# Six raw weight buffers, group results in two wide tiles, and gate operands parked by chunk in a decoder trunk on one core

## The chip, the core and the metric

The kernel runs on one core of one Trainium2 chip. The metric is the device time of one execution in microseconds (us). A core has a matrix engine (TensorE, PE in the profile; its weight loads are PEld), a vector engine (VectorE, DVE), a scalar engine (ScalarE, ACT), GpSimd (POOL) and a queue engine (SyncE, SP). Each runs its own instructions in order and waits for the others by semaphores. Here SP issues nearly all loads, POOL the copies of intermediate results to and from DRAM.

## What is computed

Two layers, each with one input projection that feeds three causal token mixers, and a merge; then a final norm. `D_MODEL` is 2048, the sequence 256 tokens. Cut to what matters:

```python
h = rms_norm(x, norm_w)
proj = h @ w_in                      # 2048 x 18064, float32
(qa, ka, va, za, qi, ki, wi, ub, zb, qc, kc, vc, zc, gates) = split(proj)
y_a = (dsa_attention(rope(qa), rope(ka), va, rope(qi), rope(ki), wi, top_k) * silu(za)) @ w_a_out
y_b = (silu(layer_norm(conv31(glu(ub)))) * silu(zb)) @ w_b_out
y_c = (stick_breaking_attention(qc, kc, vc) * silu(zc)) @ w_c_out
g = sigmoid(gates).reshape(b, s, 3, D_MODEL)
merged = g[:, :, 0] * y_a + g[:, :, 1] * y_b + g[:, :, 2] * y_c
x = x + merged @ w_out
```

## The kernel before

**Weights.** Weights stream from DRAM in units of 512 KB: `load_unit` (L179) takes a raw tile (tag `raw`, four buffers), `high` (L202) rounds it to `wh` on ACT, `low` (L206) forms the rest `wl` on DVE. The operands have three buffers each. A product then takes three passes over PE: high by high, high by low, low by high. A unit of eight or twelve matmuls of 512 columns belongs to `chunk_T` (L221), `chunk_first` (L253) or `chunk_steps` (L280).

**Slots.** Activations live in slots (tag `s8`, 128 x 2048 float32, 13 buffers; L92), smaller ones in `t4` tiles (128 x 1024, six buffers; L123). A slot is as large as two raw tiles.

**Background work.** The attention parts are generators. `background` (L142) steps at most one of the first two after each weight unit; the number that a generator yields is how many units must be loaded before its next step. `finish` runs out what is left. The taps of the depthwise convolution (L358: four products on ACT, one add on DVE) stand in a list `waiting`, from which `drain` takes one entry after each `low`; empty entries (L611) space them out.

**Stages of a layer.** Conv input and taps; stick-breaking queries, keys, values; then `stick` (L633) beside the sparse attention's projections; `index` (L708) and `attend` (L749) beside four gate chunks of branch 1 (`early`); `conv_norm` (L796) beside the gated operands. `gate` (L349) builds the gated operand of a branch in two slots, high and low parts side by side. Those of branches 2 and 0 are parked in DRAM (`park`, L790), to free their slots, and read back by `unpark` (L853).

**Merge stage.** `combine` (L859) runs over the branches in the order 1, 2, 0. Chunks of 512 gate columns are computed plainly, or read back from DRAM if they are done. The gates of branch 0 are computed by `strassen` (L935): seven products for eight, on sums of two weight blocks that `summands` (L923, the DVE add at L926) forms from raw tiles. The loop at L995 alternates: after each step of `combine` it lets the groups run on by two units of their yields. A group's four results stand in one slot, `res` (L959), and go to DRAM at L988. `turn` and the output projection follow; the rows of x that it adds are loaded on SP (L1020, L1022).

A scheduler orders each engine's instructions by the program's order, by raised priorities, and by its own estimate of when a tile is free. So the number of buffers changes the order too.

Of the kernel before, what the change touches and what calls it, by code (L numbers as in the profile page):

```python
# [8 lines left out]
F32 = mybir.dt.float32  # L9
F32R = mybir.dt.float32r  # L10
AF = mybir.ActivationFunctionType
ALU = mybir.AluOpType
# [37 lines left out]
def trunk(ctx: ExitStack, tc: tile.TileContext, x, xt, w_in, w_a, w_b, w_c, w_out,  # L50
# [37 lines left out]
    def nm(s):  # L88
        uid[0] += 1
        return f"{s}_{uid[0]}"  # L90

    def slot(dt=F32):  # L92
        return sp.tile([P, KC, S], dt, tag="s8", bufs=13, name=nm("s8"))

# [19 lines left out]
    def split_at(b, k, n, src, ts=slice(0, S)):  # L114
        split(hi(b, k, n, ts), lo(b, k, n, ts), src)
# [63 lines left out]
    def load_unit(w, k0, kn, segs, dst=None):  # L179
        n = sum(c for _, c in segs)  # L180
        raw = wp.tile([P, kn, n], F32, tag="raw", bufs=4, name=nm("raw"))
        if dst is None:
# [165 lines left out]

    def gate(c0, o, b, w, hx):  # L349
        for k in range(0, KC, 2):  # L350
            a, a3 = summed(chunk_T(w, c0 + k * P, 256, hx, KD))
            sg = sigmoid_of(a)
            with tc.high_priority():
                nc.vector.tensor_mul(a3, a3, sg)
                nc.vector.tensor_mul(a3, a3, o[:, k:k + 2, :])
                split_at(b, k, 2, a3)

    def taps(yT, cv, pr, c0, q):  # L358
# [42 lines left out]
    x1 = dp.tile([NT, P, D], F32, name="x1")  # L401
    parked = [[dp.tile([P, 4, 2, S], F32R, name=f"parked{b}{i}") for i in range(2)] for b in range(3)]
    gates = [dp.tile([NT, P, D], F32, name=f"gates{b}") for b in range(3)]
# [14 lines left out]
    for layer in range(DEPTH):  # L418
# [177 lines left out]
        for j in range(2):  # L596
# [11 lines left out]
            for q in reversed(range(TAPS)):  # L608
                waiting.append([4, [partial(taps, yT, cv, pr, j * 4, q)]])
                if q % 2:  # L610
                    waiting.append([4, []])  # L611
# [21 lines left out]
        def stick(h0, qcT=qcT, kcT=kcT, vcr=vcr, diag=diag):  # L633
# [20 lines left out]
            split(*pr_, nk[:, :768])  # L654
            yield 8
            pc = mm_tile()
# [92 lines left out]
        def attend(t, c, qaT=qaT, kaT=kaT, va=va, bias=bias):  # L749
# [24 lines left out]
            split(ph[:, :4 * n], pl[:, :4 * n], pst[:, :4 * n])  # L774
            yield 2
            po = mm_tile()
# [11 lines left out]
        for j in range(2, 4):  # L788
            early(1, j)
        def park(b, g):  # L790
            for i, v in enumerate(g):
                nc.gpsimd.dma_start(parked[b][i], v)

        finish()
        flush()
        def conv_norm(cv=cv, pr=pr):  # L796
            work = t4()
            red = [work[:, i * S:(i + 1) * S] for i in range(4)]
            sums = red[2:]
            for i in range(2):  # L800
                nc.vector.tensor_reduce(red[i], cv[:, i * 4:i * 4 + 4, :].rearrange("p c t -> p t c"), op=ALU.add, axis=AX.X)  # L801
            nc.vector.tensor_add(red[0], red[0], red[1])
            yield 3
            ps = mm_tile()
            nc.tensor.matmul(ps[:, :S], mean_w, red[0], start=True, stop=True)
            for i in range(2):
                cs = cv[:, i * 4:i * 4 + 4, :]
                nc.vector.tensor_sub(cs, cs, heads(ps[:, :S], 4))
                sq = t4()
                nc.scalar.activation(sq.rearrange("p (c t) -> p c t", c=4), cs, AF.Square)  # L810
                nc.vector.tensor_reduce(sums[i], sq.rearrange("p (c t) -> p t c", c=4), op=ALU.add, axis=AX.X)
            nc.vector.tensor_add(sums[0], sums[0], sums[1])
            yield 6
            vs = mm_tile()
            nc.tensor.matmul(vs[:, :S], mean_w, sums[0], start=True, stop=True)
            r = rsqrt_mean(vs[:, :S], 1, t4())
# [11 lines left out]
        gc = parts(KC)  # L828
        gate(O_ZC, qcT, gc, w, hx)
        park(2, gc)  # L830
        ga = parts(KC)
        gate(O_ZA, qaT, ga, w, hx)
        park(0, ga)
        finish()
# [16 lines left out]
        mx = [None] * 4  # L851

        def unpark(b):  # L853
            g = parts(KC)
            for i, v in enumerate(g):
                nc.gpsimd.dma_start(v, parked[b][i])
            return g
# [77 lines left out]
        def strassen(b, jj):  # L935
# [4 lines left out]
            for u in range(4):  # L940
# [17 lines left out]
                yield 2  # L958
            res = slot().rearrange("p a b -> p (a b)").rearrange("p (q t d) -> p q t d", q=2, t=NT)  # L959
            c11, c21, c12, c22 = res[:, 0, 0], res[:, 0, 1], res[:, 1, 0], res[:, 1, 1]  # L960
            with tc.high_priority():
# [18 lines left out]
            with tc.high_priority():  # L980
                nc.vector.tensor_add(c11, o2, c11)
                nc.vector.tensor_add(c21, o4, c21)
                nc.vector.tensor_add(c12, o3, c12)
                nc.scalar.activation(res[:, 0], res[:, 0], AF.Sigmoid)
                nc.scalar.activation(c12, c12, AF.Sigmoid)
            for q in range(2):
                j = jj * 2 + q
                nc.gpsimd.dma_start(gates[b][:, :, j * 512:(j + 1) * 512].rearrange("t p d -> p t d"), res[:, q])  # L988
            yield 3
# [5 lines left out]
        for _ in plainly:  # L995
            owed += RATE
            while owed >= 0 and fast_:
                try:
                    owed -= next(fast_[0])
                except StopIteration:  # L1000
                    fast_.pop(0)
# [126 lines left out]
```

## Time and profile before

| | us |
|---|---|
| median of three runs | 2088.27 |
| lowest, highest | 2085.84, 2090.1 |
| profiled execution, whole | 2091.38 |
| its span | 2089.6 |
| mean granted TensorE clock | 0.996 of full |

The span runs from the first to the last instruction of the program; the whole time has some 2 us more around it. A row of a list of groups gives source line, engine, operation, output and input tiles by the program's names, shape, count, then busy time and mean duration (ns), then the idle time of that engine just before and what ended it. A row of waits reads "who waited <- for whom: total us, times, longest us". L-numbers are lines of the kernel before.

### The profile page before, as it was taken

To read this page: it belongs to the slowest core of one execution; us is meant where nothing else is said; L and a number is where in the kernel's file an instruction comes from. 1 tells how busy PE (TensorE), PEld (TensorE's weight loads), DVE (VectorE), ACT (ScalarE), POOL (GpSimd) and SP (SyncE) were. 2 spreads that over 40 slices of the span, in tenths; PEclk is the share of its full clock that TensorE was granted. 3 is DMA by queue.
4 is the path that set the end of the run, shared out by engine and by line. 5 is a ranking of instruction groups with operands and counts; after the bars stand their busy time and mean duration, and the time that the engine had idled before them with its cause. 6 is when DMAs were issued, how large, how long until landed. Compare 5 with 4: busy or idle time off the path is not lost.

```text
span 2089.6 us, 29031 instructions
## 1 busy us (share of the span) xinstructions
PE 2052.1 (98%) x10942; PEld 1778.3 (85%) x10942; DVE 1595.5 (76%) x1828; ACT 1301.4 (62%) x1845; POOL 34.7 (2%) x56
## 2 busy tenths in 40 slices
PE   9999999999999999899999999999999999999998
PEld 9888889988888777788898888899888887787887
DVE  8877677798977878666577777778989678887655
ACT  6887565688655555444459875666876555555444
POOL 0000000000000000000000000000000000000000
PEclk9999999999999999999999999999999999999999
DMA  6666556655776767686666665565557766686864
GB/s 242 204 190 191 167 164 206 202 185 169 242 233 218 238 215 244 227 283 202 204 192 190 185 191 173 162 212 192 187 166 252 231 223 233 225 279 201 275 213 145
DMA packets 302044, 436.24 MB, mean 209 GB/s; under 512 B 17744, under 2 KB 182096, under 8 KB 299728
## 3 DMA queue, kind: packets, MB, share of 16 engines
q1 hardware_dynamic: 293472, 398.20, 60.0%
q0 software_dynamic: 6912, 33.56, 4.5%
q10 hardware_dynamic: 1520, 2.64, 0.4%
q8 instruction: 85, 1.39, 0.3%
q14 instruction: 55, 0.45, 0.1%
HBM read 413.37 MB, written 20.97 MB: 208 GB/s over the span
## 4 chain that ended last, share of the span: by engine, by line
PE 87%; DMA 5%; DVE 5%; issue 2%; ACT 1%; ACTq 0%; SPq 0%; DVEq 0%
PE acc L218 79%; DMA raw<-in_w_in_dram 5%; PE mm L218 4%; DVE wl L208 3%; PE mm L717 1%; ACT wh L204 1%; DVE t L926 1%; PE mm L754 1%; DVE t L801 0%; PE mm L845 0%; PE mm L672 0%; PE mm L636 0%; PE mm L779 0%; PE mm L386 0%; PE mm L658 0%
## 5 line engine op out<-in xcount | busy, mean ns | idle before, releaser
L204 ACT CAST wh<-raw 128x1024 fp32r<-128x1024 f32 (+2 forms) x712 | 740.2, 1040 | 604.7 <-PE acc L218 384.0
L208 DVE TENSOR_TENSOR wl<-raw,wh 128x1024 fp32r<-128x1024 f32 (+2 forms) x713 | 857.8, 1209 | 333.3 <-ACT wh L204 315.6
L218 PE MATMUL acc<-wh,s 128*128 128x512 f32 (+2 forms) x2688 | 652.9, 385 | 0.0
L218 PE MATMUL acc<-s,wh 128*128 128x512 f32 (+2 forms) x2912 | 645.0, 365 | 2.3 <-ACT s L503 1.7
L218 PEld LDWEIGHTS acc<-wh,s 128*128 128x128 f32 x2688 | 492.9, 189 | 96.7 <-ACT wh L204 0.5
L218 PEld LDWEIGHTS acc<-s,wh 128*128 128x128 f32 x2912 | 491.3, 190 | 63.9 <-ACT s L503 2.0
L218 PEld LDWEIGHTS acc<-s,wl 128*128 128x128 f32 x2656 | 357.5, 191 | 19.4 <-DVE wl L208 0.9
L218 PE MATMUL acc<-s,wl 128*128 128x256 f32 (+1 forms) x2656 | 366.1, 281 | 0.5 <-DVE wl L208 0.4
L218 PE MATMUL acc<-wl,s 128*128 128x512 f32 (+2 forms) x1344 | 351.9, 384 | 13.2 <-DVE wl L208 13.1
L218 PEld LDWEIGHTS acc<-wl,s 128*128 128x128 f32 x1344 | 247.2, 188 | 66.5 <-DVE wl L208 18.5
L369 ACT ACTIVATE t<-s,cst 128x255 f32<-128x255 f32 (+14 forms) x480 | 201.5, 489 | 0.2
L372 DVE TENSOR_TENSOR s<-s,t 128x1020 f32<-128x1020 f32 (+14 forms) x120 | 138.3, 1153 | 1.0 <-ACT t L369 0.5
L218 PE MATMUL mm<-wh,s 128*128 128x512 f32 x448 | 119.9, 389 | 0.0
L218 PEld LDWEIGHTS mm<-wh,s 128*128 128x128 f32 x448 | 84.0, 188 | 18.0 <-issue 0.4
L218 PE MATMUL mm<-wl,s 128*128 128x512 f32 x224 | 70.2, 394 | 7.3 <-DVE wl L208 7.3
L204 ACT CAST wh<-s 128x1024 fp32r<-128x1024 f32 x32 | 33.6, 1050 | 47.7 <-DVE s L926 28.4
L218 PEld LDWEIGHTS mm<-wl,s 128*128 128x128 f32 x224 | 41.2, 188 | 19.1 <-DVE wl L208 11.2
L926 DVE TENSOR_TENSOR s<-s,raw 128x1024 f32<-128x1024 f32 x16 | 19.6, 1226 | 46.5 <-DMA raw<-in_w_in_dram 46.5
L926 DVE TENSOR_TENSOR t<-raw,raw 128x1024 f32<-128x1024 f32 x32 | 39.1, 1222 | 16.7 <-DMA raw<-in_w_in_dram 16.7
L204 ACT CAST wh<-t 128x1024 fp32r<-128x1024 f32 x32 | 33.5, 1048 | 19.0 <-DVE t L926 10.5
L208 DVE TENSOR_TENSOR wl<-t,wh 128x1024 fp32r<-128x1024 f32 x32 | 39.0, 1219 | 1.1 <-ACT wh L204 0.7
L208 DVE TENSOR_TENSOR wl<-s,wh 128x1024 fp32r<-128x1024 f32 x32 | 38.9, 1217 | 0.0
(203 smaller groups left out, 1167.5 us busy)
## 6 DMA issues: line engine op xcount, KB each, us to landing
raw<-in_w_in_dram SPq DMA_DIRECT2D x571, 512.0 KB, 3.6
raw<-in_w_out_dram SPq DMA_DIRECT2D x64, 512.0 KB, 3.8
raw<-in_w_b_dram SPq DMA_DIRECT2D x32, 512.0 KB, 3.6
raw<-in_w_c_dram SPq DMA_DIRECT2D x32, 512.0 KB, 5.3
raw<-in_w_a_dram SPq DMA_DIRECT2D x32, 512.0 KB, 5.7
parked<-s POOLq DMA_DIRECT2D x8, 1024.0 KB, 5.5
t<-gates POOLq DMA_DIRECT2D x16, 512.0 KB, 6.4
s<-parked POOLq DMA_DIRECT2D x8, 1024.0 KB, 8.4
```

Source lines behind the costliest of these rows:

```text
L204: nc.scalar.copy(u[1], u[0])
L208: sub = nc.vector.tensor_sub(u[2], u[0], u[1].bitcast(F32))
L218: newest[0] = nc.tensor.matmul(o, lhsT, rhs, start=start, stop=stop, skip_group_check=True)
L369: nc.scalar.activation(o[:, i, :S - d], yT[:, c, :S - d], AF.Copy, scale=wq)
L372: nc.vector.tensor_add(to, to, o[:, :, :S - d])
L717: nc.tensor.matmul(ps[:, q * n:(q + 1) * n], at(qiT, hd)[:, t * P:(t + 1) * P], kiT[:, 0, :n], start=True, stop=True)
L754: nc.tensor.matmul(ps[:, q * n:(q + 1) * n], qaT[:, c * 4 + q, ts_], kaT[:, c, :n], start=True, stop=True)
L926: nc.vector.tensor_tensor(o, a_, b_, op=op)
```

## The change

Raw tiles get six buffers, slots twelve. A group's results go to two `t4` tiles. `gate` parks each pair of chunks as soon as it is formed, into one DRAM tile per branch that is laid out by chunk; `unpark` puts eight small reads on a list, of which the loop of the merge stage issues one per step. The strided reductions of `conv_norm` become adds of halves. `stick` waits 10 units, not 8, before its second step, `attend` 3, not 2, before its third. The empty entries among the taps stand after every fourth tap, not after every second.

```diff
-        return sp.tile([P, KC, S], dt, tag="s8", bufs=13, name=nm("s8"))
+        return sp.tile([P, KC, S], dt, tag="s8", bufs=12, name=nm("s8"))
...
-        raw = wp.tile([P, kn, n], F32, tag="raw", bufs=4, name=nm("raw"))
+        raw = wp.tile([P, kn, n], F32, tag="raw", bufs=6, name=nm("raw"))
...
-    def gate(c0, o, b, w, hx):
+    def gate(c0, o, b, w, hx, park=None):
         for k in range(0, KC, 2):
...
                 split_at(b, k, 2, a3)
+            if park is not None:
+                nc.gpsimd.dma_start(park[:, k:k + 2], part(b, slice(0, 2), k, 2))
...
-    parked = [[dp.tile([P, 4, 2, S], F32R, name=f"parked{b}{i}") for i in range(2)] for b in range(3)]
+    parked = [dp.tile([P, KC, 2, S], F32R, name=f"parked{b}") for b in range(3)]
...
-                if q % 2:
+                if q % 4 == 0:
                     waiting.append([4, []])
...
-            yield 8
+            yield 10
             pc = mm_tile()
...
-            yield 2
+            yield 3
             po = mm_tile()
...
-            for i in range(2):
-                nc.vector.tensor_reduce(red[i], cv[:, i * 4:i * 4 + 4, :].rearrange("p c t -> p t c"), op=ALU.add, axis=AX.X)
-            nc.vector.tensor_add(red[0], red[0], red[1])
+
+            def fold(w_, first, second):
+                w4 = w_.rearrange("p (c t) -> p c t", c=4)
+                nc.vector.tensor_add(w4, first, second)
+                nc.vector.tensor_add(w_[:, :512], w_[:, :512], w_[:, 512:])
+                nc.vector.tensor_add(w_[:, :S], w_[:, :S], w_[:, S:2 * S])
+                return w_[:, :S]
+
+            s1 = fold(work, cv[:, :4, :], cv[:, 4:, :])
             yield 3
...
-        gate(O_ZC, qcT, gc, w, hx)
-        park(2, gc)
+        gate(O_ZC, qcT, gc, w, hx, parked[2])
         ga = parts(KC)
-        gate(O_ZA, qaT, ga, w, hx)
-        park(0, ga)
+        gate(O_ZA, qaT, ga, w, hx, parked[0])
...
+        back = []
+
         def unpark(b):
             g = parts(KC)
-            for i, v in enumerate(g):
-                nc.gpsimd.dma_start(v, parked[b][i])
+            back.extend(partial(nc.gpsimd.dma_start, g[k // 4][:, k % 4], parked[b][:, k]) for k in range(KC))
             return g
...
-            res = slot().rearrange("p a b -> p (a b)").rearrange("p (q t d) -> p q t d", q=2, t=NT)
-            c11, c21, c12, c22 = res[:, 0, 0], res[:, 0, 1], res[:, 1, 0], res[:, 1, 1]
+            res = [t4().rearrange("p (t d) -> p t d", t=NT) for _ in range(2)]
+            c11, c21, c12, c22 = (r[:, t, :] for r in res for t in range(NT))
...
         for _ in plainly:
             owed += RATE
+            if back:
+                back.pop(0)()
```

The squares in `conv_norm` are summed by `fold` in the same way.

**The readbacks, on POOL, in the merge stage of layer 0.** `s` are slots, `parked` and `gates` the tiles in DRAM, `t` the t4 tiles. Before:

```order
L856 DMA s_1081_6695<-parked_87 128x2048
L856 DMA s_1082_6696<-parked_88 128x2048
L988 DMA gates_89<-s_1136_6948 128x2x512 x2
L871 DMA t_1401_8233<-gates_89 128x2x512
L871 DMA t_1415_8312<-gates_89 128x2x512
L856 DMA s_1335_7891<-parked_83 128x2048
L856 DMA s_1336_7892<-parked_84 128x2048
L988 DMA gates_89<-s_1315_7789 128x2x512 x2
```
Now (line numbers of the changed kernel):

```order
L998 DMA s_1081_6696<-parked_85 128x512 x4
L998 DMA s_1082_6697<-parked_85 128x512 x4
L988 DMA gates_86<-t_1136_6955 128x2x512
L988 DMA gates_86<-t_1137_6956 128x2x512
L998 DMA s_1337_7900<-parked_83 128x512 x4
L998 DMA s_1338_7901<-parked_83 128x512 x4
L871 DMA t_1403_8248<-gates_86 128x2x512
L871 DMA t_1417_8327<-gates_86 128x2x512
```
Each readback of a slot is now four transfers that stand side by side; those of branch 0 (`parked_83`) moved ahead of the two reads of finished gates.

**The end of the attention stage in layer 0, on DVE.** `cv` is slot 76; `pl` is the low half of the transposed attention weights, for the last two of four `attend`. Before:

```order
L326 TENSOR_TENSOR pl_4947<-mm_4937,ph_4946 128x1024
L372 TENSOR_TENSOR s_76_720<-s_76_720,t_780_4956 128x4x226
L208 TENSOR_TENSOR wl_5060<-raw_5058,wh_5059 128x1024
L801 TENSOR_REDUCE t_793_5032<-s_76_720 128x256 x2
L326 TENSOR_TENSOR pl_4984<-mm_4974,ph_4983 128x1024
L802 TENSOR_TENSOR t_793_5032<-t_793_5032 128x256
```
Now:

```order
L799 TENSOR_TENSOR t_793_5029<-s_76_717 128x1024
L208 TENSOR_TENSOR wl_5057<-raw_5055,wh_5056 128x1024
L800 TENSOR_TENSOR t_793_5029<-t_793_5029 128x512
L801 TENSOR_TENSOR t_793_5029<-t_793_5029 128x256
L326 TENSOR_TENSOR pl_4968<-mm_4958,ph_4967 128x1024
L208 TENSOR_TENSOR wl_5079<-raw_5077,wh_5078 128x1024
L326 TENSOR_TENSOR pl_4993<-mm_4983,ph_4992 128x1024
```
The reductions and a tap stood between the two `pl`; the adds now stand ahead of the first, and only one low half of a weight unit is left between them.

**The loads on SP before the output projection of layer 0.** Before:

```order
L193 DMA raw_8236<-in_w_a_dram 128x2x512
L193 DMA raw_8254<-in_w_a_dram 128x2x512
L1020 DMA t_1471_8594<-in_x_dram 128x2x512
L193 DMA raw_8272<-in_w_a_dram 128x2x512
L1020 DMA t_1501_8771<-in_x_dram 128x2x512
```
Now:

```order
L193 DMA raw_8251<-in_w_a_dram 128x2x512
L193 DMA raw_8269<-in_w_a_dram 128x2x512
L193 DMA raw_8287<-in_w_a_dram 128x2x512
L193 DMA raw_8305<-in_w_a_dram 128x2x512
L1022 DMA t_1473_8609<-in_x_dram 128x2x512
L193 DMA raw_8330<-in_w_a_dram 128x2x512
L1022 DMA t_1503_8786<-in_x_dram 128x2x512
```
Two more raw loads stand ahead of the first x load. The t4 tiles that the x loads fill are now those of the last group's results, so each waits until its store to `gates` has landed.

More of the change, by code (lines that the diff above doesn't have):

```diff
@@ L789, in trunk @@
             early(1, j)
-        def park(b, g):
-            for i, v in enumerate(g):
-                nc.gpsimd.dma_start(parked[b][i], v)
         finish()
@@ L797, in conv_norm @@
             work = t4()
-            red = [work[:, i * S:(i + 1) * S] for i in range(4)]
-            sums = red[2:]
-            for i in range(2):
-                nc.vector.tensor_reduce(red[i], cv[:, i * 4:i * 4 + 4, :].rearrange("p c t -> p t c"), op=ALU.add, axis=AX.X)
-            nc.vector.tensor_add(red[0], red[0], red[1])
+            def fold(w_, first, second):
[5 more added lines that the diff above has]
+            s1 = fold(work, cv[:, :4, :], cv[:, 4:, :])
             yield 3
             ps = mm_tile()
-            nc.tensor.matmul(ps[:, :S], mean_w, red[0], start=True, stop=True)
+            nc.tensor.matmul(ps[:, :S], mean_w, s1, start=True, stop=True)
+            sq = [t4().rearrange("p (c t) -> p c t", c=4) for _ in range(2)]
             for i in range(2):
@@ L808, in conv_norm @@
                 nc.vector.tensor_sub(cs, cs, heads(ps[:, :S], 4))
[L809 to L812, printed above, removed]
+                nc.scalar.activation(sq[i], cs, AF.Square)
+            s2 = fold(work, *sq)
             yield 6
             vs = mm_tile()
-            nc.tensor.matmul(vs[:, :S], mean_w, sums[0], start=True, stop=True)
+            nc.tensor.matmul(vs[:, :S], mean_w, s2, start=True, stop=True)
             r = rsqrt_mean(vs[:, :S], 1, t4())
@@ L851, in trunk @@
         mx = [None] * 4
+        back = []
         def unpark(b):
             g = parts(KC)
-            for i, v in enumerate(g):
-                nc.gpsimd.dma_start(v, parked[b][i])
+            back.extend(partial(nc.gpsimd.dma_start, g[k // 4][:, k % 4], parked[b][:, k]) for k in range(KC))
             return g
@@ L983, in strassen @@
                 nc.vector.tensor_add(c12, o3, c12)
-                nc.scalar.activation(res[:, 0], res[:, 0], AF.Sigmoid)
+                nc.scalar.activation(res[0], res[0], AF.Sigmoid)
                 nc.scalar.activation(c12, c12, AF.Sigmoid)
@@ L987, in strassen @@
                 j = jj * 2 + q
-                nc.gpsimd.dma_start(gates[b][:, :, j * 512:(j + 1) * 512].rearrange("t p d -> p t d"), res[:, q])
+                nc.gpsimd.dma_start(gates[b][:, :, j * 512:(j + 1) * 512].rearrange("t p d -> p t d"), res[q])
             yield 3
```

## The prediction

> **What bounds the kernel now.** I read the page first, for the engine that is never idle, then the waits of that engine, then the stretches in which those waits lie, then the instructions of one such stretch.
>
> ```profile
> span 2089.6 us, 29031 instructions
> PE 2052.1 (98%) x10942; PEld 1778.3 (85%) x10942; DVE 1595.5 (76%) x1828; ACT 1301.4 (62%) x1845; POOL 34.7 (2%) x56
> PE 87%; DMA 5%; DVE 5%; issue 2%; ACT 1%; ACTq 0%; SPq 0%; DVEq 0%
> ```
> TensorE (PE) is busy 98% of the span, and the chain that ended last runs over it for 87%. The change adds and removes no matmul, so all that it can win is PE's idle time, 37.5 us, and what that idle time costs beside it. The profiled execution took 2091.4 us, 1.8 us more than its span, and lies 3.1 us above the median of the three runs, 2088.3; I make the sum against 2091.4 and take the 3.1 us off at the end.
>
> The list of waits over the whole span says for what PE stood still:
>
> ```profile
> PE acc L218 <- DVE wl L208: 13.5, 10, 4.1
> PE mm L218 <- DVE wl L208: 7.3, 7, 1.6
> DVE s L926 <- DMA raw<-in_w_in_dram: 55.6, 25, 8.3
> SPq L193 <- DVE wl L208: 1487.3, 657, 10.2
> ```
> Columns are total, times and longest. PE waited 17 times, 20.8 us in all, for the low half of a weight unit (`wl`). Behind it VectorE (DVE) stood 55.6 us at the sums of two weight blocks (L926) because a raw block had not landed. And the queue that issues the raw loads (SP) spent 1487 us waiting for DVE to be done with an older raw tile: loads go out late because no raw buffer is free, not because the transfers are slow.
>
> Where those waits lie, by stretches (length, then busy time and instructions of PE, PEld, DVE, ACT, POOL, then granted clock, DMA share and GB/s):
>
> ```profile
> 240.00:330.00 90.00, 88.70 (x550) 80.24 (x549) 68.61 (x89) 61.41 (x81) 0.00 (x0) 1.00 0.55 167
> 430.00:540.00 110.00, 108.85 (x540) 91.75 (x539) 98.69 (x139) 88.33 (x163) 3.47 (x5) 1.00 0.58 182
> 675.00:895.00 220.00, 208.47 (x898) 168.40 (x897) 173.85 (x165) 114.53 (x117) 5.30 (x8) 0.99 0.70 232
> 1280.00:1370.00 90.00, 89.14 (x554) 81.02 (x553) 69.41 (x90) 60.62 (x80) 0.00 (x0) 1.00 0.57 173
> 1470.00:1575.00 105.00, 103.85 (x516) 87.47 (x514) 94.51 (x129) 84.04 (x157) 2.92 (x4) 1.00 0.58 181
> 1710.00:1930.00 220.00, 210.96 (x911) 170.88 (x911) 175.61 (x166) 115.69 (x118) 5.20 (x8) 0.99 0.70 232
> ```
> The merge stage, where the plain chunks and the seven-product groups alternate, holds 11.5 us of idle PE in the first layer and 9.0 in the second: all of the 20.8 us. The stick-breaking and sparse-attention stages hold 1.3 + 1.15 + 0.9 + 1.15 = 4.5 us. The other 12 us of the 37.5 lie outside these stretches, most at the start and behind the last matmul, and I leave them as they are.
>
> The longest wait, in order of time (start, length, engine, operation, in brackets the idle time before it):
>
> ```profile
> 834.93 0.57 POOL L856 DMA_DIRECT2D s<-parked  x1 [25.34 <-PE mm L218]
> 837.83 0.37 SPq L193 DMA_DIRECT2D raw<-in_w_in_dram  x1
> 839.01 0.55 POOL L856 DMA_DIRECT2D s<-parked  x1 [3.51 <-PE mm L218]
> 840.77 0.37 SPq L193 DMA_DIRECT2D raw<-in_w_c_dram  x1
> ...
> 849.03 1.23 DVE L926 TENSOR_TENSOR s<-s,raw 128x1024 f32<-128x1024 f32 x1 [8.29 <-DMA raw<-in_w_in_dram]
> 851.44 2.04 PE L218 MATMUL acc<-wl,s 128*128 128x512 f32 x4 [4.12 <-DVE wl L208]
> ...
> 1885.39 1.78 PE L218 MATMUL acc<-wl,s 128*128 128x512 f32 x4 [3.15 <-DVE wl L208]
> ```
> Two parked tiles of 1 MB each are read back just when three raw loads are under way; the block issued at 837.83 is what L926 waits for until 849.03, and PE loses 4.12 us. The second layer has the like, 3.15 us. DMA was then full:
>
> ```profile
> 834.00:842.00 8.00, 8.00 (x37) 6.62 (x36) 6.17 (x6) 5.49 (x7) 1.11 (x2) 1.00 0.80 282
> 842.00:846.00 4.00, 4.00 (x19) 3.33 (x18) 0.00 (x0) 0.59 (x2) 0.00 (x0) 1.00 1.06 402
> 850.00:854.00 4.00, 2.56 (x6) 2.08 (x7) 3.97 (x6) 1.19 (x2) 0.00 (x0) 0.69 0.37 115
> 854.00:860.00 6.00, 6.00 (x26) 4.86 (x26) 3.48 (x5) 3.37 (x4) 0.00 (x0) 0.92 0.64 186
> 1884.00:1888.00 4.00, 2.61 (x7) 2.09 (x8) 3.96 (x6) 1.14 (x2) 0.00 (x0) 0.72 0.39 126
> 1888.00:1892.00 4.00, 4.00 (x17) 3.23 (x16) 3.35 (x4) 1.69 (x3) 0.00 (x0) 0.86 0.80 239
> ```
> It moved 402 GB/s, against 232 on average over the stage. After this wait, and its like in the second layer, the granted clock fell: 4 x 0.31 + 6 x 0.08 = 1.7 us lost, and 4 x 0.28 + 4 x 0.14 = 1.7.
>
> **The change, part by part.** *Six raw buffers.* One load more or less is not the point; each may now go out two units earlier. A unit of 12 matmuls of 512 columns takes 12 x 227 ns = 2.7 us by
>
> ```profile
> 1986.29 10.90 PE acc L218 x48
> L218 PE MATMUL acc<-wh,s 128*128 128x512 f32 (+2 forms) x2688 | 652.9, 385 | 0.0
> raw<-in_w_in_dram SPq DMA_DIRECT2D x571, 512.0 KB, 3.6
> ```
> (10.90 / 48 = 0.227 us), so two units are some 5.4 us of lead on top of today's. The longest of the 17 waits is 4.1 us, so a lead of 5.4 us covers every one by itself. A wait costs more than its idle time: a matmul is shown busy for 0.385 us but is followed by the next after 0.227, so 0.16 us of each wait is hidden as busy, 17 x 0.16 = 2.7 us. Sum of the term: 20.8 + 2.7 + 3.4 for the clock = 26.9 us. I take four fifths of it, 21.5 us. What is late next is the chain raw, sum, cast (ACT), low half (DVE): in the merge stage DVE is busy 173.85 of 220 us and runs in order, and the new order puts several L926 one place earlier, ahead of the low half of the unit before. A block that is still late then holds back that unit too. Bounds: nothing won at the one end, 26.9 us at the other.
>
> The Trainium skill's page TensorE: Matmul & The Clock Gate ("What's actually happening") has the array drop to half rate after an idle window of about 3.4 us. The trace drops after the wait of 4.12 us and also after that of 3.15; by the page alone the second layer's 1.7 us would not be won, and the total would be 2064.
>
> *Slots from 13 to 12, group results in two t4 tiles.* A slot is as large as two raw buffers, so SBUF stays full. The result of a group held the 13th slot; it now holds two of six t4 tiles from the middle of a group until its store to DRAM has landed. While they are held, the sums of the next group have four t4 tiles, two per round, so that only the third round asks for a held one. A round is four products of six matmuls, 4 x 1.36 us, and the 3.5 plain units that the loop lets in between, 3.5 x 2.7: 15 us. Two rounds, 30 us, stand against a store of
>
> ```profile
> gates<-s POOLq DMA_DIRECT2D x8, 512.0 KB, 7.4
> s<-parked POOLq DMA_DIRECT2D x8, 1024.0 KB, 8.4
> raw<-in_w_in_dram SPq DMA_DIRECT2D x17, 256.0 KB, 2.8
> ```
> so I cost it at nothing. Without that cover each of the eight stores would stop DVE, with ACT and SP behind it, for up to 7.4 us. The first x loads of the output projection also reuse such a tile and wait on SP for the last store; SP's raw loads are queued behind them. By the order six raw units are issued by then, four of them not yet used, 11 us against 7.4: nothing.
>
> *Parking by chunk, read back in eight pieces.* Same bytes, 8 issues for 2. The pieces are handed out one per step, but nothing on POOL ties them to the step: POOL is idle, and they go as soon as their slot is free, at the same two places as now. POOL issues one in 0.55 us, so four take 2.2 us. With one slot fewer the first readback waits for the branch-1 operands on both halves. It is used after eight plain units and 16 units of a group, about 34 us later. Eight pieces one after another at 2.8 us are 22 us, two whole ones 17: hidden, zero. Whether the smaller pieces let the raw loads through better is not shown; from nothing to the 4 us that the burst costs, and these are in the first term already.
>
> *Sums by a tree, waits of 10 and 3 units, taps closer together.* In the attention stage PE waits for `pl`:
>
> ```profile
> 504.84 3.98 DVE L801 TENSOR_REDUCE t<-s 128x256 f32<-128x1024 f32 x2
> 508.74 1.21 DVE L326 TENSOR_TENSOR pl<-mm,ph 128x1024 fp32r<-128x1024 f32 x1
> 510.01 0.50 PE L779 MATMUL mm<-pl,t 128*128 128x512 f32 x1 [1.15 <-DVE pl L326]
> 258.24 0.51 PE L658 MATMUL mm<-ph,upper_r 128*128 128x512 f32 x1 [1.30 <-ACT ph L325]
> ```
> The two strided reductions stand in front of `pl` on DVE for 3.98 us. The three adds that replace them are a full tile, a half and a quarter of one; by the 1.21 us of `pl`, itself a full tile, an estimate of 1.21 x 1.75 = 2.1 us. In the new order they stand before both `pl`, not between. The stick-breaking wait goes because L658 moves two units back, one of them of 2.7 us. Idle 4.5 us and some six waits of 0.16: 5.4; four fifths, 4.3 us. Bound below: with the longer wait the last pieces run together at the end of the stage, one unit of 2.7 us apart, against a chain of subtract, exponential and mask on tiles of 768 columns, each at most three quarters of L926's 1.23: 2.8 us. At worst 1 us more per layer.
>
> The taps stand in four of five units instead of two of three. ACT:
>
> ```profile
> 66.00:100.00 34.00, 34.00 (x196) 29.90 (x196) 26.66 (x25) 34.00 (x69) 0.00 (x0) 1.00 0.65 198
> L204 ACT CAST wh<-raw 128x1024 fp32r<-128x1024 f32 x12 | 12.5, 1039 | 0.0
> L369 ACT ACTIVATE t<-s,cst 128x254 f32<-128x254 f32 (+12 forms) x51 | 21.5, 497 | 0.0
> ```
> Here (rows of this stretch alone) 12 casts and 51 tap products, a tap in every unit, filled ACT for all 34 us, and PE did not wait. Four in five for longer is no more than that: zero. If the cover of the three `wh` tiles runs out: a tapped unit asks ACT for 1.04 + 4 x 0.42 us, and the six other instructions of the stretch, each half a cast as an estimate, for 0.26 more per unit, 2.99 in all against 34 / 12 = 2.83 of PE. That is 0.16 too much, over 40 units and two layers 13 us.
>
> Sum: 21.5 + 4.3 = 25.8; 2091.4 - 25.8 = 2065.6; less 3.1, **2062 us**.
>
> **Rivals.** *The burst stays* (0.14): the loads go out earlier but meet the same readbacks, and DVE's order keeps half of the waits: 13.5 us won, 2075. For it: 402 GB/s is no more than the engines give. Against: the need is 232 x 220 / 207 = 247 GB/s.
>
> *Small pieces are slow and their readers wait* (0.05): 5.6 us more per readback, four readbacks, 22 us: 2084. The Trainium skill's DMA: Bandwidth & Descriptors ("Measured") asks for 1 MiB and more per transfer and would speak for this one; the trace has 256 KB at 2.8 us and 1 MB at 8.4, but no 256 KB from POOL.
>
> *The change doesn't do what it says* (0.03): PE's waits come from DVE's order, not from the raw buffers; only the attention stages gain: 2084 to 2088. Against it stands SP's row.
>
> *ACT becomes the bound among the taps* (0.02): 13 us given back, 2075.
>
> *Slower* (0.06): the held t4 tiles. If a store lands behind raw traffic so late that L926 waits for it, DVE stands, raw buffers are not freed and PE starves. It decides from 30 us behind the store's issue; 7.4 us for each of eight stores would be 59 us, half of them 30 us on top of the gain: 2092 and up to 2121.
>
> **How the numbers follow.** The forecast, 0.70, lies between all of 32.3 us won (2056, and 2053 with the spread of the runs) and some 20 us (2068). To hold eight in ten the range goes on over the halved gain and ACT's price: 2053 to 2078. A measurement of this kernel tells some 0.2%, 4 us, from no change: faster by more than that 0.70 + 0.14 + 0.02 = 0.86; within it 0.08; slower 0.06.
>
> **What would show it.** In the new profile SP's total wait for `wl` may stay long, but DVE's 55.6 us at L926 should fall under 15, PE's two rows for `wl` from 20.8 to some 4, the merge stretches to 216 of 220 us and more, and no stretch there have a clock under 0.95. `pl` should no longer stand behind L801. I am wrong if L926 waits for a store, if PE waits for `wh` between 66 and 180 us, or if the readbacks' pieces show as PE's releaser.

## The result, and the profile after

| | us |
|---|---|
| before, median of four runs | 2088.23 |
| changed kernel, median of four runs (lowest to highest) | 2075.77 (2073.81 to 2078.17) |
| ratio, with its 95% interval | 0.9941 (0.9924 to 0.9959) |
| span of the profiled execution | 2076.4 |

The changed kernel is 12.5 us faster, a little under half of the 26 forecast. The time lies near the upper end of the stated range; the likeliest case did not come. The page of the changed kernel (span, busy time, and the chain that ended last by engine):

```profile
span 2076.4 us, 29086 instructions
PE 2049.5 (99%) x10942; PEld 1779.3 (86%) x10942; DVE 1590.2 (77%) x1828; ACT 1302.2 (63%) x1845; POOL 51.6 (2%) x88
PE 60%; DMA 3%; DVE 2%; issue 1%; ACT 0%; SPq 0%; DVEq 0%; ACTq 0%
```
PE is still idle for 26.9 us. Its stretches, as in the table of before (the same stages, moved by the time won; the last two rows are one place in the merge stage):

```profile
238.50:328.50 90.00, 90.00 (x559) 81.96 (x558) 69.08 (x89) 64.29 (x86) 0.00 (x0) 1.00 0.58 179
429.00:539.00 110.00, 110.00 (x546) 92.84 (x545) 88.70 (x131) 76.92 (x130) 4.87 (x7) 1.00 0.62 193
674.00:894.00 220.00, 213.27 (x926) 173.78 (x925) 175.50 (x165) 118.02 (x120) 13.73 (x23) 0.99 0.74 241
1270.00:1360.00 90.00, 90.00 (x562) 82.19 (x561) 70.30 (x90) 63.13 (x85) 0.00 (x0) 1.00 0.58 181
1460.00:1565.00 105.00, 105.00 (x520) 88.53 (x519) 84.21 (x122) 73.67 (x127) 3.48 (x5) 1.00 0.60 190
1700.00:1920.00 220.00, 212.40 (x919) 172.61 (x919) 173.88 (x164) 117.05 (x118) 13.02 (x22) 0.99 0.74 237
852.00:853.00 1.00, 1.00 (x4) 0.81 (x3) 1.00 (x2) 0.34 (x1) 0.00 (x0) 0.50 0.24 33
854.00:856.00 2.00, 2.00 (x8) 1.55 (x8) 0.85 (x2) 0.53 (x1) 0.00 (x0) 0.77 0.93 278
```
The stick-breaking and attention stages have no idle PE any more. The merge stages keep 6.7 and 7.6 us of the 11.5 and 9.0, and after one wait in each of them the clock is still halved (the last two rows show it in the first layer). For the waits, first a list of before that the prediction did not show, then the same and the rows of PE after the change:

```profile
DVE t L926 <- DMA raw<-in_w_in_dram: 16.7, 16, 2.5
ACT wh L204 <- DMA raw<-in_w_in_dram: 46.0, 37, 3.9
```
```profile
DVE s L926 <- DMA raw<-in_w_in_dram: 34.8, 26, 5.5
DVE t L926 <- DMA raw<-in_w_in_dram: 24.6, 13, 3.9
ACT wh L204 <- DMA raw<-in_w_in_dram: 2.3, 2, 1.7
PE mm L218 <- DVE wl L208: 13.8, 13, 2.5
PE acc L218 <- DVE wl L208: 0.9, 2, 0.5
SPq L193 <- DVE wl L208: 1516.7, 655, 9.7
```
This is the puzzle of the case in six rows. The casts on ACT hardly wait for blocks of `w_in` any more: 46.0 us became 2.3. The two new buffers did give loads a lead. But the sums on DVE (L926) still stand 59.4 us for theirs, against 72.3, and PE 14.7 us for low halves, against 20.8.

I sum PE's **late starts**: for two matmuls that follow each other, the time between their starts above what the same shapes take undisturbed, over all gaps more than 40 ns too long. They hold the idle time, the part of it that is hidden because a matmul is shown busy for longer than it holds up the next, and what the clock cost. Before they were 29.6 us in the two merge stages, 2.9 at the stick-breaking steps and 3.6 at the attention steps; after, 22.0, 0 and 1.5. So the merge stages gave some 7.7 us, the other two 5.1, and that is nearly all of the gain (the span of these two profiles fell by 13.2).

The place of the longest wait in the changed kernel, DVE's instructions in order of time, and then PE's:

```profile
840.40 1.22 DVE L208 TENSOR_TENSOR wl<-raw,wh 128x1024 fp32r<-128x1024 f32 x1
847.02 1.23 DVE L926 TENSOR_TENSOR s<-s,raw 128x1024 f32<-128x1024 f32 x1 [5.41 <-DMA raw<-in_w_in_dram]
848.17 0.68 DVE L966 TENSOR_TENSOR t<-mm,t 128x512 f32<-128x512 f32 x1
848.77 1.22 DVE L208 TENSOR_TENSOR wl<-s,wh 128x1024 fp32r<-128x1024 f32 x1
```
```profile
846.52 1.07 PE L218 MATMUL mm<-wh,s 128*128 128x512 f32 x4
850.04 0.74 PE L218 MATMUL mm<-wl,s 128*128 128x512 f32 x2 [2.45 <-DVE wl L208]
```
PE waits for the low half that DVE makes at 848.77. Its high half had long been there, by ACT's row:

```profile
841.73 1.05 ACT L204 CAST wh<-s 128x1024 fp32r<-128x1024 f32 x1 [1.66 <-PE acc L218]
```
It is queued behind a sum that serves a later unit and has no data yet. The program's order on DVE at this place, before and then after the change (`raw_7914` and `raw_7922` are the same block of weights, `wl_7848` and `wl_7857` the same low half; rows of other lines are left out):

```
L208 TENSOR_TENSOR wl_7848<-s_1227_7383,wh_7847 128x1024
L926 TENSOR_TENSOR s_1250_7489<-s_1250_7489,raw_7914 128x1024
L208 TENSOR_TENSOR wl_7859<-raw_7857,wh_7858 128x1024
L208 TENSOR_TENSOR wl_7878<-raw_7875,wh_7877 128x1024
L208 TENSOR_TENSOR wl_7898<-raw_7896,wh_7897 128x1024
L208 TENSOR_TENSOR wl_7917<-raw_7914,wh_7916 128x1024
L208 TENSOR_TENSOR wl_7928<-s_1250_7489,wh_7927 128x1024
```
```
L926 TENSOR_TENSOR s_1251_7497<-s_1251_7497,raw_7922 128x1024
L208 TENSOR_TENSOR wl_7857<-s_1228_7391,wh_7856 128x1024
L208 TENSOR_TENSOR wl_7868<-raw_7866,wh_7867 128x1024
L208 TENSOR_TENSOR wl_7887<-raw_7884,wh_7886 128x1024
L208 TENSOR_TENSOR wl_7905<-raw_7903,wh_7904 128x1024
L208 TENSOR_TENSOR wl_7925<-raw_7922,wh_7924 128x1024
L208 TENSOR_TENSOR wl_7936<-s_1251_7497,wh_7935 128x1024
```
Call the **distance** of a sum the number of low halves that PE needs earlier and that stand behind it on DVE: 4 here before, 5 now, and the one that it has overtaken is the one that PE waits for. Single sums moved by 1 to 5 places. Over the 64 sums the distance was 1 to 4, mean 2.3 (1 in 20, 2 in 10, 3 in 28, 4 in 6), and is 3 to 7, mean 5.3. Two buffers more, and the sums stand three places earlier, on average, in a queue that runs in order.

### The profile page after: what moved, and what is told of

Its sections match the earlier page's. It is cut to its first block, busy times and chain, and to the rows that moved or that the text cites. A ratio compares the mean times of both kernels' runs of the same rounds, so it can differ in the third digit from the quotient of the medians.

```text
span 2076.4 us, 29086 instructions
## 1 busy us (share of the span) xinstructions
PE 2049.5 (99%) x10942; PEld 1779.3 (86%) x10942; DVE 1590.2 (77%) x1828; ACT 1302.2 (63%) x1845; POOL 51.6 (2%) x88
## 4 chain that ended last, share of the span: by engine, by line
PE 60%; DMA 3%; DVE 2%; issue 1%; ACT 0%; SPq 0%; DVEq 0%; ACTq 0%
PE acc L218 52%; PE mm L218 5%; DMA raw<-in_w_in_dram 3%; DVE wl L208 1%; PE mm L719 1%; DVE t L926 0%; PE mm L844 0%; PE mm L756 0%; PE mm L781 0%; PE mm L388 0%; PE mm L674 0%; PE mm L638 0%; ACT wh L204 0%; PE mm L773 0%; PE mm L660 0%
## 5 line engine op out<-in xcount | busy, mean ns | idle before, releaser
L208 DVE TENSOR_TENSOR wl<-raw,wh 128x1024 fp32r<-128x1024 f32 (+2 forms) x713 | 858.0, 1209 | 320.1 <-ACT wh L204 305.3
L218 PE MATMUL acc<-wh,s 128*128 128x512 f32 (+2 forms) x2688 | 652.5, 385 | 0.0
L218 PE MATMUL acc<-s,wh 128*128 128x512 f32 (+2 forms) x2912 | 645.2, 365 | 2.3 <-ACT s L505 1.9
L218 PEld LDWEIGHTS acc<-wh,s 128*128 128x128 f32 x2688 | 492.3, 188 | 96.3 <-ACT wh L204 0.3
L218 PEld LDWEIGHTS acc<-s,wh 128*128 128x128 f32 x2912 | 491.0, 190 | 63.8 <-ACT s L505 2.2
L218 PEld LDWEIGHTS acc<-s,wl 128*128 128x128 f32 x2656 | 357.9, 191 | 19.7 <-DVE wl L208 0.9
L218 PE MATMUL acc<-s,wl 128*128 128x256 f32 (+1 forms) x2656 | 366.7, 281 | 0.5 <-DVE wl L208 0.4
L218 PE MATMUL acc<-wl,s 128*128 128x512 f32 (+2 forms) x1344 | 350.6, 383 | 0.5 <-DVE wl L208 0.5
L218 PEld LDWEIGHTS acc<-wl,s 128*128 128x128 f32 x1344 | 248.5, 189 | 50.4 <-DVE wl L208 1.4
L218 PE MATMUL mm<-wh,s 128*128 128x512 f32 x448 | 119.8, 389 | 0.0
L218 PEld LDWEIGHTS mm<-wh,s 128*128 128x128 f32 x448 | 84.4, 188 | 17.7
L218 PE MATMUL mm<-wl,s 128*128 128x512 f32 x224 | 70.7, 397 | 13.8 <-DVE wl L208 13.8
L218 PEld LDWEIGHTS mm<-wl,s 128*128 128x128 f32 x224 | 40.9, 188 | 27.5 <-DVE wl L208 20.0
L926 DVE TENSOR_TENSOR t<-raw,raw 128x1024 f32<-128x1024 f32 x32 | 39.1, 1222 | 24.6 <-DMA raw<-in_w_in_dram 24.6
L208 DVE TENSOR_TENSOR wl<-s,wh 128x1024 fp32r<-128x1024 f32 x32 | 39.0, 1220 | 3.5 <-ACT wh L204 3.5
L926 DVE TENSOR_TENSOR s<-s,raw 128x1024 f32<-128x1024 f32 x16 | 19.6, 1225 | 26.8 <-DMA raw<-in_w_in_dram 26.8
L208 DVE TENSOR_TENSOR wl<-t,wh 128x1024 fp32r<-128x1024 f32 x32 | 39.0, 1218 | 0.5 <-ACT wh L204 0.5
```

Source lines behind the costliest of these rows:

```text
L208: sub = nc.vector.tensor_sub(u[2], u[0], u[1].bitcast(F32))
L218: newest[0] = nc.tensor.matmul(o, lhsT, rhs, start=start, stop=stop, skip_group_check=True)
L926: nc.vector.tensor_tensor(o, a_, b_, op=op)
```

## The experiments

Each expectation is quoted as it stood before its run. All times are medians, all ratios to the kernel before, run beside it on the same chip.

| run | raw buffers | distance | us | ratio (95%) | late starts, merge |
|---|---|---|---|---|---|
| changed kernel again | 6 | 3 to 7 | 2076.36 | 0.9946 (0.9934 to 0.9959) | 19.4 |
| raw4_in_after | 4 | 1 to 4 | 2080.74 | 0.9953 (0.9941 to 0.9965) | 22.6 |
| raw6_in_before | 6 | 3 to 7 | 2079.04 | 0.9942 (0.9930 to 0.9954) | 19.7 |
| noread_in_after | 6 | 3 to 7 | 2066.27 | 0.9881 (0.9868 to 0.9894) | 9.4 |
| whole_in_after | 6 | 3 to 7 | 2073.84 | 0.9933 (0.9920 to 0.9947) | 16.0 |
| raw4_whole_in_after | 4 | 1 to 4 | 2083.13 | 0.9975 (0.9965 to 0.9986) | 27.0 |
| tie2_in_after | 6 | 1 | 2055.15 | 0.9829 (0.9816 to 0.9841) | 0.1 |
| tie4_in_after | 6 | 3 | 2054.92 | 0.9844 (0.9826 to 0.9861) | 0.1 |
| tie4_whole_in_after | 6 | 3 | 2055.42 | 0.9849 (0.9835 to 0.9862) | 0.1 |
| tie5_in_after | 6 | 4 (3 in 4 of 64) | 2061.36 | 0.9874 (0.9861 to 0.9888) | 6.4 |
| tie6_in_after | 6 | 5 (less in 16) | 2078.53 | 0.9955 (0.9940 to 0.9970) | 22.0 |
| tie4_raw5_in_after | 5 | 3 (2 in 6) | 2063.93 | 0.9889 (0.9875 to 0.9902) | 6.5 |
| tie2_in_before | 4 | 1 (0 in 4) | 2079.20 | 0.9960 (0.9947 to 0.9974) | 15.4 |
| tie2_raw4_in_after | 4 | 1 (0 in 4) | 2073.77 | 0.9926 (0.9912 to 0.9940) | 15.9 |

For comparison, the changed kernel in the result above has 0.9941 and 22.0 us, the kernel before 29.6 us. The late starts come from one profile each; the changed kernel's two, 22.0 and 19.4, show how far such sums scatter. The runs come from four chips, and the kernel before took 2086.75 to 2090.45 us on them, so differences of some 2 us between runs of two chips are read from the ratios.

**The buffers alone, and all but the buffers.**

```diff
-        raw = wp.tile([P, kn, n], F32, tag="raw", bufs=6, name=nm("raw"))
+        raw = wp.tile([P, kn, n], F32, tag="raw", bufs=4, name=nm("raw"))
```


> The changed kernel with four raw buffers again, all else of the change kept. By order: the merge stages lose what they won (16.1 + 13.2 us of late matmul starts before, 10.3 + 11.6 after: 7.4 us), the attention stages keep theirs (5.3 us): 2075.8 + 7.4 = 2083, between 2081 and 2086; the rows of PE for the low half go back to some 20 us. If the pieces or the tree made the gain and the buffers nothing: 2076.

The other run, raw6_in_before, makes in the kernel before the edits of the change to `raw` (6), `s8` (12) and `res`, and no more. It is called the buffers alone below, though slots and results moved with them.

> The kernel before with six raw buffers, twelve slots and the group results in two t4 tiles, and no other part of the change: readbacks whole, norms by reductions, old waits, old taps. If gains add up: 2088.2 - 7.4 = 2081, between 2079 and 2084, and PE still waits 12 to 16 us for the low half. If buffers only help together with the small pieces: 2086 or more.

The buffers alone win 11.4 us against the kernel before beside them, where 7.4 were expected; the 2079.04 us lie in the range only because that chip was 2 us slower. The rest alone wins 9.7, where some 5 were expected (2080.74, just under the range). Both together win no more than the buffers alone: in the merge stages the gains do not add (late starts of 29.6 us before, 22.6 with the rest, 19.7 with the buffers, 22.0 and 19.4 with both). The count of buffers alone also sets the order: the distances of raw4_in_after are those of before, those of raw6_in_before are those of the changed kernel, one by one.

**Hold the order on DVE.** The most telling run ties each sum behind a low half that was traced shortly before it:

```diff
             sub = nc.vector.tensor_sub(u[2], u[0], u[1].bitcast(F32))
+        lows.append(sub)
...
-            with tc.high_priority():
+            with tc.high_priority(), tc.issue_after(lows[-2].ins):
                 nc.vector.tensor_tensor(o, a_, b_, op=op)
```


> The changed kernel, but each sum of two weight blocks (L926) is ordered behind the low half of the unit before the last, so that it stands ahead of 1 earlier low half on DVE instead of 3 to 7. Theory of the order (the new lead went to the casts, while DVE's queue moved the sums forward by as much, and each sum still meets a block that has just been asked for): PE's waits for the low half fall from 14.3 to under 4 us, the idle time at the sums from 59 us to under 15, and the time to 2076 - 10.3 - about 2 hidden - about 2 of clock = 2062, between 2058 and 2066. Theory of the burst (readbacks and loads share the DMA engines, the order matters little): 2072 to 2076, with the two longest waits left as they are.

**Take the readbacks away.**

```diff
-            back.extend(partial(nc.gpsimd.dma_start, g[k // 4][:, k % 4], parked[b][:, k]) for k in range(KC))
+            back.extend(partial(nc.gpsimd.memset, g[k // 4][:, k % 4].bitcast(F32), 0.5) for k in range(KC))
```


> The changed kernel with no readback of the parked operands: POOL fills the same slots with a constant at the same places, so 4 MB per execution in four bursts less on the DMA engines; the products of branches 2 and 0 then have a constant in place of the gated values. Theory of the order: only the waits beside the readbacks shrink (late starts of 1.9 + 4.3 us in the first layer, 2.6 + 4.4 in the second at most), the others (some 8 us) stay: 2066 to 2073. Theory of the burst: nearly all waits for the low half go, under 3 us left: 2060 to 2064.

The held order (tie2_in_after) took all of it: 2055.15 us, below even the range. Its page (chain), its waits of PE above 0.3 us and of its sums (L929 is L926, L221 L218, L210 L208), and its merge stages:

```profile
PE 99%; DVE 1%; DMA 0%; ACT 0%; issue 0%; ACTq 0%
```
```profile
PE acc L221 <- ACT s L508: 1.9, 1, 1.9
PE mm L548 <- DVE eps L71: 1.1, 1, 1.1
PE acc L221 <- DVE wl L210: 0.4, 1, 0.4
DVE s L929 <- DMA raw<-in_w_in_dram: 0.2, 1, 0.2
```
```profile
674.00:894.00 220.00, 220.00 (x972) 182.18 (x971) 182.22 (x171) 122.68 (x125) 14.47 (x24) 1.00 0.82 263
1690.00:1910.00 220.00, 220.00 (x972) 182.19 (x971) 181.72 (x169) 123.34 (x125) 14.47 (x24) 1.00 0.81 258
```
PE is busy all of 220 us at full clock, with every readback in place and DMA at 263 GB/s, where the first layer had 232 before and 241 after the change. So the burst by itself does not bind. In the scheduler's order it does stretch the waits: without the readbacks (noread_in_after) the late starts fall from 22.0 or 19.4 us to 9.4, and the gain over the changed kernel is 12.5 us by the ratios (0.9941 to 0.9881). The time, 2066.27 us, is at the edge of what the order's theory allowed, and by the ratio it is as short as the burst's theory had it. The waits fit neither: half of PE's remain, where the burst's theory left under 3 us.

```profile
PE mm L218 <- DVE wl L208: 5.0, 7, 1.7
PE acc L218 <- DVE wl L208: 2.0, 3, 0.9
```
Taking the readbacks away thus helps in part; holding the order leaves nothing for them to cost.

**The order alone, with four buffers, and other distances.** The same edit in the kernel before; then with `lows[-4]` and `lows[-6]` in the changed kernel.

> The kernel before (four raw buffers, whole readbacks, reductions) with each sum of two weight blocks ordered behind the low half of the unit before the last, so that it stands ahead of 0 or 1 earlier low half instead of 1 to 4. If the order alone makes the waits: the 29.3 us of late starts in the merge stages go, the 5.4 of the attention stages stay: 2090 - 29 = 2061, between 2058 and 2066. If the buffers are needed as well (the casts of the merge stage begin 0.1 us behind a landing with four buffers): some waits are left, 2068 to 2082.

> The changed kernel with each sum ordered behind the fourth last low half: 3 earlier low halves stand behind it on DVE, the distance that was the commonest with four buffers. If the two new buffers give two units of lead when the distance is held: no or nearly no wait for the low half, 2055 to 2060. If any distance above 1 makes waits: 2064 to 2074.

> The changed kernel with each sum ordered behind the sixth last low half, where the order lets it: 5 earlier low halves behind it in most places, 3 or 4 in the rest, and never 6 or 7. By the order: nearly the waits of the changed kernel, 2068 to 2077. If what helped at a distance of 1 was something else than the distance (any fixed place on DVE): 2055 to 2060.

At a distance of 3 nothing is lost; at 5 all is back (2078.53 us, 1.5 above the range expected). The held place by itself thus helps nothing: the distance does. tie6_in_after, PE and the sums:

```profile
PE mm L221 <- DVE wl L210: 11.9, 10, 3.0
PE acc L221 <- DVE wl L210: 4.1, 5, 1.4
DVE s L929 <- DMA raw<-in_w_in_dram: 43.5, 28, 5.0
DVE t L929 <- DMA raw<-in_w_in_dram: 31.1, 14, 4.2
```
The order alone, with four buffers, won 9.4 us, a third of the 29 that were expected if it were the whole cause: 2079, not 2061. The rows of tie2_in_before show what is late there:

```profile
ACT wh L204 <- DMA raw<-in_w_in_dram: 49.8, 40, 2.7
PE acc L221 <- ACT wh L204: 5.2, 6, 1.9
DVE s L929 <- DMA raw<-in_w_in_dram: 7.3, 5, 3.0
```
Now the sums wait for 16.0 us (7.3 here and 8.7 into `t`), not 72.3; the casts still wait, and PE waits for high halves: of the 15.4 us of late starts some 14 stand at a matmul that reads one.

**How much lead, and whether pieces matter.** `lows[-5]` with six buffers; `lows[-4]` with five; `lows[-4]` with whole readbacks; and whole readbacks in the changed kernel:

```diff
-            back.extend(partial(nc.gpsimd.dma_start, g[k // 4][:, k % 4], parked[b][:, k]) for k in range(KC))
+            for i, v in enumerate(g):
+                nc.gpsimd.dma_start(v, parked[b][:, 4 * i:4 * i + 4])
```


> The changed kernel once more, on the same chip as the three beside it, as their common base: 0.994 of the kernel before, 2075 to 2079.

> The changed kernel with each sum ordered behind the fifth last low half, so that 4 earlier low halves stand behind it on DVE. At a distance of 3 there was no wait for the low half (2055), at 5 there were as many as in the changed kernel (2078). If six buffers give a fixed lead that a distance of 4 has just used up: between the two, 2058 to 2072. If the waits come only where sums are spread unevenly: 2055.

> The changed kernel with sums ordered at a distance of 3 and five raw buffers. With one buffer less the lead should be that of six buffers at a distance of 4, the same as the run beside it within 4 us; if five are enough: 2055.

> The changed kernel with sums ordered at a distance of 3, and the parked tiles read back whole. If pieces or whole matters only to loads that have no lead: 2053 to 2057, as with pieces. If the burst of whole readbacks still outlasts the lead: 2058 to 2064.

> The changed kernel with each parked tile read back whole, in two transfers of 1 MB at once, and still parked by chunk. Six buffers alone won 11.4 us in the kernel before, where readbacks are whole, and the attention stages win 5.3 beside that. If these add up and the eight pieces cost the difference: 2072 to 2074 where the changed kernel has 2076 to 2078 on the same chip. If pieces or not is nothing: 2076 to 2078. If the pieces help against the burst: 2080 or more.

One buffer less costs about what one place of distance costs: 2063.9 and 2061.4, with intervals that overlap. With five and six buffers and a held order, buffers less distance tells the time, as a lead of the sum: 5 and 3 give 2055, 2 gives 2061 to 2064, 1 gives 2078. With four buffers it does not: there 4 less 1 is 3 as well, and the two runs take 2074 and 2079, because the casts are late. With a lead of 3, pieces or whole is nothing (2054.9, 2055.4). In the changed kernel as it stands, 2073.84 against 2075.77 and 2076.36, with intervals that overlap, leaves it open.

**Four buffers, with whole readbacks, and with the order held.** These are raw4_in_after with the edit to whole readbacks, and with `lows[-2]`.

> The changed kernel with four raw buffers and with whole readbacks. If the pieces won the 7 us in the merge stages with four buffers: late starts there back to 29 us, 2088 less the 5 of the attention stages, 2082 to 2085. If the results in t4 tiles (or chance) won them: 22 us late, 2078 to 2081.

> The changed kernel with sums ordered at a distance of 1 and four raw buffers. If the two buffers are worth in the held order what tie2_in_before shows (late starts of 15 us in the merge stages against 0): 2055 + 15 = 2070, between 2066 and 2074, with PE waiting for the high half where a cast meets its load. If pieces make up for two buffers: 2055 to 2062.

With four buffers and the old order, whole readbacks cost 4.6 us by the ratios (0.9975 against 0.9953) and 2.4 by the times; the two runs come from two chips, and the intervals meet at 0.9965. The late starts say the same (27.0 whole, 22.6 in pieces), from one profile each. So the pieces probably won most of what the rest of the change won in the merge stages; it is not shown beyond the noise.

The worth of the two buffers shows. With the order left to the scheduler it depends on the readbacks: in pieces, 0.9953 to 0.9941 or 0.9946, some 2 us; whole, 0.9975 to 0.9933 in the changed kernel, 9 us, and 12 by the ratio of raw6_in_before. With the order held it is 0.9926 to 0.9829, 20 us.

## Why the prediction was half right

**What bounds.** Right: all of the gain came from PE's idle time. The chain is now 99% PE in the best of the runs.

**Six raw buffers, 21.5 us forecast, 7.7 us won** (in the merge stages, by the whole change). The step that failed is the sentence "The longest of the 17 waits is 4.1 us, so a lead of 5.4 us covers every one by itself." It gives the lead to every reader of a raw block. The casts got it: in the merge stage of the first layer, by the landing of each load and the first instruction that reads its tile, 29 of 66 casts began within 0.15 us of the landing before, and none of 63 after (median 7.4 us). The sums did not: 19 of 23 before, 19 of 26 after. In tie2_in_after it is 1 of 17, with a median of 3.7 us. The order took the lead away: it moved the sums forward by three low halves while the loads gained two. That this is the cause, tie4_in_after shows: six buffers with the sums at a distance of 3 leave 0.1 us of late starts. The step saw the mechanism ("ahead of the low half of the unit before. A block that is still late then holds back that unit too") and mis-sized it: "one place earlier" is right for the place of the longest wait, but the count over all 64 sums, which could be had without a run, says three, and a fifth of the term was too little for it. The prediction's own signs failed with it: DVE stood 34.8 us at the first row of L926, not under 15; PE waited 14.7 us for low halves, not some 4; the merge stretches hold 213.3 and 212.4 us of busy PE, not 216; and the clock fell to 0.50.

That SP's wait would stay long was right, and for that reason its row was no proof: 1487 us before, 1517 after. "Loads go out late because no raw buffer is free" was true of before, and not the whole cause.

**Pieces and readbacks, zero.** Not contradicted with six buffers: no wait of PE names them, and whole or in pieces stays within the noise. But the price that the prediction gave the burst, from nothing to 4 us, was too small: in the changed kernel the readbacks cost 12.5 us by the ratios. A piece took 5.5 us to land (median), where the prediction had put 2.8. The Trainium skill's DMA: Bandwidth & Descriptors ("Measured") asks for 1 MiB and more in a transfer. These runs do not bear that out as a rule for this kernel: with a lead, 256 KB and 1 MB differ by 0.5 us, and with four buffers, where loads meet the readback, the pieces were if anything better.

**Slots, results in t4 tiles.** Zero, as costed: L926 has raw loads alone as its releaser, never a store.

**Norm sums and the longer waits, 4.3 us forecast, 5.1 won in their stages.** The stick-breaking waits are gone, but not, or not mainly, because `stick` waits 10 units. With the buffers alone and the old 8 units they are gone too; with four buffers and 10 units more than half of the idle time stays. The stretch from 240 to 330 us had 88.70 us of busy PE before; in raw6_in_before and in raw4_in_after:

```profile
240.00:330.00 90.00, 89.94 (x557) 81.50 (x556) 69.26 (x90) 61.91 (x81) 0.00 (x0) 1.00 0.58 176
240.00:330.00 90.00, 89.03 (x551) 80.85 (x550) 69.42 (x90) 62.72 (x84) 0.00 (x0) 1.00 0.57 171
```
So this part belongs to the raw buffers. The attention steps are as the prediction has them: their stretch from 430 us on keeps its 1.15 us of idle PE with the buffers alone and has none with the rest alone. There `pl` stands behind its cast, no longer behind the reduction (attention stage of the first layer, DVE, in order of time):

```profile
502.57 0.42 DVE L801 TENSOR_TENSOR t<-t 128x256 f32<-128x256 f32 x1
504.01 1.22 DVE L326 TENSOR_TENSOR pl<-mm,ph 128x1024 fp32r<-128x1024 f32 x1 [1.02 <-ACT ph L325]
508.68 1.23 DVE L326 TENSOR_TENSOR pl<-mm,ph 128x1024 fp32r<-128x1024 f32 x1 [2.32 <-ACT ph L325]
```
**Taps, zero.** Right: the stretch in which they stand closest has no idle PE.

```profile
66.00:180.00 114.00, 114.00 (x656) 100.34 (x655) 91.28 (x86) 108.49 (x210) 0.00 (x0) 1.00 0.63 191
```
**The rivals.** *The burst stays* named the time, 2075, and both halves of the cause: the readbacks that the loads still meet, and DVE's order. That the time agrees is partly luck: its 13.5 us are half of the term of the raw buffers, without the attention stages, and that term gave 7.7 and the attention stages 5.1. It put the readbacks first; tie2_in_after, with the readbacks left, shows that the order comes first. *The change doesn't do what it says* had the right reason, "PE's waits come from DVE's order, not from the raw buffers", and was dismissed with SP's row; tie2_in_before shows that the reason holds only together with the buffers, since with four of them the casts are late instead. The price of small pieces, 22 us, and the slower rival did not occur.

What stays open: the taps, the parking by chunk and the t4 results were not taken out one by one, and whole or in pieces in the changed kernel as it stands was not told apart. Best of all runs are the changed kernel with the sums held, at a distance of 1 or 3: 2055 us, 1.6 to 1.7% under the kernel before.

## What to carry to other kernels

More buffers lengthen the lead of a load in full only for the readers that keep their place: where a scheduler orders an in-order engine, count how many earlier instructions each waiting reader overtakes, before and after, and take that off the lead. A wait that moves from one engine to another when an order is fixed (here from sums to casts) says that two limits stood together; then only both edits at once show what either is worth. Where an engine stands on data that it need not have yet, tie the instruction behind the work that is due first.

## What the runs showed of the hardware

The clock was cut after shorter waits than those of before. In the changed kernel a wait of 2.45 us (until 850.04) was followed by a granted clock of 0.50; in tie6_in_after a wait of 2.50 us (until 850.52) was not, and one of 2.99 us (until 1880.93) was. So the length of a wait does not decide it alone here.

What does decide shows in stretches of one length. In every trace of this case the cuts behind such waits last 3.41 us, and those of one trace start whole multiples of 3.41 us apart. Here are the stretches of this raster around the three waits, first two of the changed kernel, then four of tie6_in_after (the second number behind the window is PE's busy time, the third from the end the clock):

```profile
848.11:851.52 3.41, 1.48 (x6) 1.16 (x7) 2.91 (x4) 2.63 (x4) 0.00 (x0) 1.00 0.06 23
851.52:854.93 3.41, 3.41 (x9) 2.65 (x8) 2.46 (x3) 1.87 (x2) 0.00 (x0) 0.50 0.61 177
846.20:849.61 3.41, 1.82 (x9) 1.16 (x7) 2.10 (x3) 0.24 (x1) 0.00 (x0) 1.00 0.54 199
849.61:853.02 3.41, 2.50 (x11) 1.97 (x12) 2.91 (x3) 3.23 (x4) 0.00 (x0) 1.00 0.00 0
1877.03:1880.44 3.41, 0.92 (x5) 0.41 (x3) 2.52 (x3) 0.66 (x2) 0.00 (x0) 1.00 0.45 169
1880.44:1883.85 3.41, 2.92 (x7) 2.34 (x8) 2.91 (x4) 2.80 (x3) 0.00 (x0) 0.50 0.09 10
```
The wait of 2.45 us left PE 1.48 us of work in one stretch, and the next was cut. The wait of 2.50 us fell on two stretches and left 1.82 and 2.50 us; neither was followed by a cut. Over the 16 traces (from 50 to 2040 us) all 15 stretches of the raster with at most 1.56 us of busy PE were followed by a cut, and none of those with 1.71 us or more. So PE's share in one such stretch decides, and the border lies between 46 and 50% here; a wait of 2.5 us costs some 1.7 us or nothing, by where it falls (1.7 us: half of a cut of 3.41).

The Trainium skill's TensorE: Matmul & The Clock Gate ("What's actually happening") has the drop behind an idle window of about 3.4 us, and calls the window free-running. The length and the raster agree with the traces. If an idle window is one without any work, the traces do not bear that out: PE was busy for up to 46% of the stretch before a cut.
